# A hybrid decoder step: first tiles group by group, HGRN sample tokens as 32-column weight tiles, triangle steps later in the emitted order

## The chip, the cores and the metric

The kernel runs on one core of one Trainium2 chip. The metric is the device time of one execution in microseconds (us). A core has five engines that run their own instruction streams in order: PE (TensorE, matrix products; PEld is its weight load), DVE (VectorE), ACT (ScalarE), POOL (GpSimd) and SP (SyncE, which here only issues transfers). They wait for each other through semaphores.

## The reference

One layer of a decoder with three kinds of mixing heads side by side, for 256 prompt tokens and 8 sample sequences of 8 tokens each (T = 320 columns). All in float32.

```
hn   = rms_norm(x, norm_mix)                      # x: 320 tokens x 2048
proj = hn @ w_in                                  # 2048 x 6656: 52 output tiles of 128 columns
y_rw = rwkv7_mix(proj[:, :2560], ...)             # 12 heads x 64, as 6 pairs; needs a triangular inverse per 64-token chunk
y_hg = hgrn2_mix(proj[:, 2560:5632], ...)         # 6 heads, state 128 x 128
y_lr = rglru_mix(proj[:, 5632:], ...)             # 512 channels
x    = x + concat(y_rw, y_hg, y_lr) @ w_out       # 16 output tiles
hn   = rms_norm(x, norm_ffn)
gate, val = split(hn @ ffn_w_up)                  # 2 x 5632 columns, conv of width 3 on the gate
x    = x + (silu(conv(gate)) * val) @ ffn_w_down
y    = rms_norm(x, norm_final)

# inside hgrn2_mix, per head and chunk:
o_inter = einsum('bthk,bhkv->bthv', q * exp(b), S)    # the state's share; for sample tokens S is the given state_hgrn
```

## The kernel before

**Products.** Channels lie on the 128 partitions, tokens in the free dimension. A float32 product is made of three: the weight and the input are each split into a rounded high part (ACT, `S.copy` or `S.activation`) and the rest (DVE, the difference), called wh, wl and xh, xl. A tile of 128 output columns takes, for each 128 rows of the input, wh with xh (line 198), wh with xl (line 199) and wl with xh (line 205). A weight chunk is eight such 128 x 128 blocks, 512 KB, so a chunk makes 24 of these large matmuls and an input-projection tile (two chunks) makes 48. Large matmuls of 320 columns are 9600 of PE's matmuls; all others (the "aux" ones) belong to the heads and are plain float32, for which the trace shows two records per matmul.

**Order.** `gemm` emits a tile's matmuls; after every fourth step and every chunk it calls `tick`, which advances generator functions that wait in queues (`QUEUES`): "r" for the chunks of an RWKV pair (`rwkv_chunks`), "f" for its operands, "n" for its norm, "h" for an HGRN head, "l" for the RG-LRU, "y" for the splits ahead of the output projection. A generator yields a number of estimated microseconds (`L_FRONT`, `L_SUB`, `L_EV` ...) to wait on an emission clock that large matmuls (`GEMM_COST`) and aux steps (`AUX_COST`) push on. So these numbers set where in the instruction streams the small work stands; the scheduler of the framework then makes each engine's order from it, and may let neighbours pass each other unless `tc.keep_in_program_order` forbids it. `ORDER` runs pair 0, head 0, pair 1, head 1 and so on, then the RG-LRU pairs.

**Start.** SP loads half chunks of the first weights (`raw`) and most of the 16 input tiles xr; POOL loads every fourth xr, then prm (all small parameters) and cst (constant matrices). ACT's split of an input tile scales it by a column of prm (`nmix`). The first two output tiles (`ps_0`, `ps_1` in `aux_r` buffers: decay/learning-rate and gate inputs of RWKV) are computed in two halves of eight steps. The squares of xr are summed for the RMS norm, one matmul with ones (line 370) adds over partitions, and `rstd` (a square root, then a reciprocal on DVE) scales every projected tile when it is read out of PSUM. Tiles are read by `shifted` (lines 335 to 352, through one `ext` buffer) or `projected`. The projection tiles use two `acc` buffers in turn; `aux_r` has four buffers, `aux_h` two.

**RWKV pair.** `shifted` tiles k, r, v; `rwkv_operands` (first matmuls line 446, then 466); `rwkv_chunks` with the score matmuls (lines 540, 550), masks into mt1 and mt2 on DVE, and the inverse of the 16 x 16 diagonal triangles: mt1 is written to DRAM (`dn`), its diagonal blocks are read as 40 rows (`n16`), 30 small DVE steps (lines 573, 575) build the inverse, which goes by DRAM (`du`) into `Us`. The next reader of `Us` is the transposition at line 648, emitted `L_SUB` after the step ahead of it. `rwkv_norm` (lines 787, 794, 804) follows.

**HGRN head.** `hgrn_steps` makes decayed scores in growing block sizes (lines 871, 875, copied into `at` by DVE at lines 872, 876), then the output `ps_o`:

```
PE.matmul(ps_o[:, TP:T], vt[0:64, 2, :], at[0:64, TP:T], start=True, stop=False, skip_group_check=True)
for m in range(SB):
    PE.matmul(ps_o[:, TP + m * ST:TP + (m + 1) * ST], s0[m // 4][:, m % 4, :], eb[:, m * ST:(m + 1) * ST],
              start=False, stop=True, skip_group_check=True)
```

The first (line 963) is the sample tokens' own share, on 64 rows of the array. The loop (line 965) adds the states' share: for each of the eight sequences its 128 x 128 state is the weight and its eight tokens `eb` (q times exp of the decay) are the moving columns.

Of the kernel before, what the change touches and what calls it, by code (L numbers as in the profile page):

```python
# [66 lines left out]
def kernel(ctx: ExitStack, tc: tile.TileContext, i: dict, o: dict):  # L67
# [200 lines left out]
    for k in range(NK):
        if k % 4 == 0:
            split_weights(2 * (k // 8), slice(k % 8, k % 8 + 4))  # L270
        a, b = split_tiles(k)
        split(xr[k], a, b, pc("nmix", k))
        xh.append(a)
        xl.append(b)
        if k % 4 == 3:
            split_weights(2 * (k // 8) + 1, slice(k % 8 - 3, k % 8 + 1))
# [80 lines left out]
    def rwkv_front():  # L357
        ssq = et("ext", T)

        def squares(ks):  # L360
            for k in ks:
                add_square(ssq, xr[k], k, lambda: rp.tile([P, T], F32, tag="c", name="sq", bufs=BC))
# [7 lines left out]
        PE.matmul(ps_n[:, :T], ones, ssq, start=True, stop=True)  # L370
# [1038 lines left out]
```

## Time and profile before

| what | value |
|---|---|
| median of 3 runs | 1648.94 us (1647.66 to 1649.54) |
| profiled execution, its own time | 1651.69 us |
| its span, first to last instruction | 1649.9 us |
| mean granted TensorE clock | 0.992 |
| PE busy | 1613.8 us, 98% of the span, 11508 matmul records |
| DVE, ACT, POOL busy | 983.7, 827.9, 154.8 us |
| DMA | 238.86 MB, mean 145 GB/s |

A record of PE shows from when a matmul ran to its modelled end; records overlap, so the distance from one start to the next is what a matmul costs in a stream. "idle before" is the time that an engine stood still ahead of an instruction, with what ended it. The granted clock is 1.00 or 0.50 in any short stretch.

### The profile page before, as it was taken

The numbers are of one execution on the slowest core, as the hardware profiler recorded it, in microseconds if no ns is written. First come the engines' busy times: TensorE is split into PE (matmuls) and PEld (weight loads), VectorE is DVE, ScalarE is ACT, GpSimd is POOL, SyncE is SP. The second block draws the span as 40 slices with busy tenths as digits, with TensorE's granted clock in tenths as the row PEclk, the third lists the DMA queues.
The fourth block names the chain that finished last, engine by engine and source line by source line (L and its number), as shares of the span: only waits on it lengthen the run. The fifth ranks groups of instructions, "written<-read, shape, count | busy, mean of one in ns | idle before, by whom it ended". The sixth has DMA issues, their size and how long they took to land.

```text
span 1649.9 us, 29024 instructions
## 1 busy us (share of the span) xinstructions
PE 1613.8 (98%) x11508; PEld 1567.1 (95%) x11508; DVE 983.7 (60%) x1952; ACT 827.9 (50%) x1293; POOL 154.8 (9%) x369
## 2 busy tenths in 40 slices
PE   7999999999999999999999999999999999999996
PEld 7888998999899899999999999999999999999996
DVE  7777777877777656555555554343455555554444
ACT  7675767676766874443434433323343343344441
POOL 2001010101012210010000000000000000010000
PEclk9999999999999999999999999999999999999998
DMA  7434443434343455444444544555544444455553
GB/s 255 151 123 123 121 132 113 131 113 131 113 128 120 149 158 165 147 157 154 149 146 152 151 146 144 151 154 151 153 150 146 152 154 151 146 155 153 146 153 105
DMA packets 87103, 238.86 MB, mean 145 GB/s; under 512 B 16568, under 2 KB 30312, under 8 KB 86968
## 3 DMA queue, kind: packets, MB, share of 16 engines
q1 hardware_dynamic: 82072, 221.67, 44.1%
q0 software_dynamic: 4896, 15.35, 2.9%
q8 instruction: 90, 1.47, 0.4%
q14 instruction: 45, 0.37, 0.1%
HBM read 225.62 MB, written 11.37 MB: 144 GB/s over the span
## 4 chain that ended last, share of the span: by engine, by line
PE 90%; DVE 3%; DMA 3%; ACT 3%; issue 1%; SPq 0%; DVEq 0%; ACTq 0%
PE acc L205 27%; PE acc L198 27%; PE acc L199 26%; DMA U<-du 1%; PE aux_r L665 1%; PE aux_h L875 1%; DVE wl L174 1%; PE aux_h L965 1%; DMA xr<-in_xT 1%; DMA du<-u 1%; PE aux_r L198 0%; PE aux_h L998 0%; PE aux_r L199 0%; ACT wh L173 0%; DVE x L1234 0%
## 5 line engine op out<-in xcount | busy, mean ns | idle before, releaser
L173 ACT CAST wh<-raw 128x1024 fp32r<-128x1024 f32 (+2 forms) x412 | 421.1, 1023 | 518.9 <-PE acc L199 315.8
L198 PE MATMUL acc<-xh,wh 128*128 128x320 f32 x2208 | 668.4, 316 | 3.2 <-DVE ext L342 3.2
L199 PE MATMUL acc<-xl,wh 128*128 128x320 f32 x2208 | 658.0, 311 | 0.0
L174 DVE TENSOR_TENSOR wl<-raw,wh 128x1024 fp32r<-128x1024 f32 (+2 forms) x412 | 489.5, 1189 | 238.5 <-ACT wh L173 109.0
L198 PEld LDWEIGHTS acc<-xh,wh 128*128 128x128 f32 x2208 | 416.8, 189 | 10.9 <-issue 7.8
L199 PEld LDWEIGHTS acc<-xl,wh 128*128 128x128 f32 x2208 | 417.4, 189 | 2.1
L205 PE MATMUL acc<-xh,wl 128*128 128x320 f32 x2208 | 382.5, 314 | 0.2 <-DVE wl L174 0.2
L205 PEld LDWEIGHTS acc<-xh,wl 128*128 128x128 f32 x2208 | 337.9, 190 | 4.2 <-issue 1.0
L198 PE MATMUL acc<-hh,wh 128*128 128x320 f32 x704 | 208.2, 311 | 0.0
L199 PE MATMUL acc<-hl,wh 128*128 128x320 f32 x704 | 207.9, 308 | 0.0
L198 PEld LDWEIGHTS acc<-hh,wh 128*128 128x128 f32 x704 | 132.4, 188 | 0.0
L199 PEld LDWEIGHTS acc<-hl,wh 128*128 128x128 f32 x704 | 132.2, 188 | 0.0
L205 PE MATMUL acc<-hh,wl 128*128 128x320 f32 x704 | 118.9, 309 | 0.0
L1196 POOL COPY ncch<-fe 128x18 f32<-128x18 f32 x44 | 49.6, 1127 | 653.4 <-DVE fe L1195 653.4
L205 PEld LDWEIGHTS acc<-hh,wl 128*128 128x128 f32 x704 | 107.1, 188 | 0.0
L1206 DVE TENSOR_TENSOR fv<-acc,rstd 128x320 f32<-128x320 f32 x44 | 21.6, 492 | 98.1 <-PE acc L205 98.1
L1194 DVE TENSOR_TENSOR fe<-acc,rstd 128x256 f32<-128x256 f32 x44 | 18.7, 425 | 99.2 <-PE acc L205 99.2
L214 ACT CAST hh<-fv 128x320 fp32r<-128x320 f32 x44 | 20.3, 461 | 96.9 <-DVE fv L1208 96.9
L198 PE MATMUL acc<-yhl,wh 128*128 128x320 f32 x224 | 66.2, 310 | 0.5 <-ACT yhl L214 0.5
L199 PE MATMUL acc<-yhl,wh 128*128 128x320 f32 x224 | 66.2, 309 | 0.0
L1201 DVE SCALAR_TENSOR_TENSOR fc<-fe,prm,fc 128x336 f32<-128x336 f32 x88 | 49.8, 565 | 1.6
L1199 ACT ACTIVATE fc<-fe,prm 128x336 f32<-128x336 f32 x44 | 29.5, 669 | 35.1 <-DVE fe L1195 35.1
(406 smaller groups left out, 1650.5 us busy)
## 6 DMA issues: line engine op xcount, KB each, us to landing
raw<-in_w_up SPq DMA_DIRECT2D x176, 512.0 KB, 3.5
raw<-in_w_in SPq DMA_DIRECT2D x100, 512.0 KB, 3.7
raw<-in_w_dn SPq DMA_DIRECT2D x64, 512.0 KB, 3.6
raw<-in_w_out SPq DMA_DIRECT2D x32, 512.0 KB, 3.8
raw<-in_w_dn SPq DMA_DIRECT2D x32, 384.0 KB, 3.4
out_s_hgrn<-hs POOLq DMA_DIRECT2D x12, 256.0 KB, 3.8
hs<-in_hs POOLq DMA_DIRECT2D x10, 256.0 KB, 3.8
x<-in_xT POOLq DMA_DIRECT2D x16, 160.0 KB, 2.8
```

Of the source, the lines that this page charges most:

```text
L173: S.copy(wh[:, ks, :], raws[n][:, ks, :])
L174: V.tensor_tensor(wl[:, ks, :], raws[n][:, ks, :], wh[:, ks, :].bitcast(F32), op=ALU.subtract)
L198: PE.matmul(ps[:, :T], wh[:, k, :], xh[k0 + k], start=st, stop=False)
L199: PE.matmul(ps[:, :T], wh[:, k, :], xl[k0 + k], start=False, stop=False)
L205: PE.matmul(ps[:, :T], wl[:, k, :], xh[k0 + k], start=False, stop=en)
L214: S.copy(xh, src)
L665: PE.matmul(ps[q, b * 64:(b + 1) * 64], lhs[q, b, q], r[q], start=True, stop=True)
L1194: V.tensor_tensor(e[:, 2:258], ps[:, 0:TP], rstd[:, 0:TP], op=ALU.mult)
L1196: G.tensor_copy(ncch[:, j], e[:, 248:EX].rearrange("p (b s) -> p b s", s=10)[:, :, 8:10])
L1199: S.activation(c[:, 0:N], e[:, 0:N], AF.Identity, scale=pc("fw", 3 * j), bias=pc("fb", j))
L1201: V.scalar_tensor_tensor(c[:, 0:N], e[:, m:m + N], pc("fw", 3 * j + m), c[:, 0:N], op0=ALU.mult, op1=ALU.add)
L1206: V.tensor_tensor(val, ps[:, :T], rstd, op=ALU.mult)
```

## The change

1. **Input.** All 16 xr come through SP's queue in groups of four, each group between the halves of the weight chunks that use it; the raw buffer of chunk 3 is taken from another pool. The nmix columns of prm get a small load of their own on ACT's queue at the very start; prm and cst themselves are loaded from ACT's queue after the second and the third group. What reads prm early (`omu`, `hgrn_bounds`, `lru_rates`) stands later in the program.
2. **First tiles.** `first_tiles` makes the first two tiles group by group: for four input tiles all 12 matmuls of tile 0, then all 12 of tile 1. Three float32 matmuls on a tile of zeros (`NIDLE`) stand ahead of them. The squares are spread between the groups. After the first tiles comes pair 0's k tile, and only then the norm's matmul. Pair 0's v tile uses an `aux_r` buffer.
3. **HGRN sample tokens.** `eb` is now four weight tiles of 32 columns (16 tokens of two sequences, and 16 zero columns). Each multiplies the two states of its sequences side by side (256 moving columns) into 32 partitions of PSUM. DVE picks each token's own state's half with two masked operations (`bm2`) into `oi`; one matmul with a selection matrix (`sel`) adds it transposed to `ps_o`. The tokens' own share uses all 128 rows.
4. **Emission.** `L_SUB` goes from 5.0 to 13.5; pair 0's operands start `L_FIRST` = 11 later and end `L_FIRST_OPS` = 4 later; the norm's first wait is `L_NORM` = 2.5 instead of 1.5.
5. **Stores.** The 16 last stores of yT alternate between ACT's and SP's queue.

```
+    idle = rp.tile([P, T], F32, tag="c", name="idle", bufs=BC)
+    V.memset(idle, 0.0)
+    ps_i = aux_h()
+    for n in range(NIDLE):
+        PE.matmul(ps_i[:, :T], idle[:, 0:P], idle, start=True, stop=True)
     S.activation(warm, eps_norm, AF.Sqrt)
+    nmix = cp.tile([P, NK], F32, tag="nmix", name="nmix")
+    S.dma_start(out=nmix, in_=i["prm"][:, PRM["nmix"]:PRM["nmix"] + NK])
-    for k in range(NK):
-        if k % 4 == 0:
-            load(2 * (k // 8), slice(k % 8, k % 8 + 4))
-        t = yp.tile([P, T], F32, tag=f"y{k}", name="xr")
-        (G if k % 4 == 3 else SY).dma_start(out=t, in_=i["xT"][k])
-        if k == 0:
-            G.dma_start(out=prm, in_=i["prm"])
...
-    G.dma_start(out=cst, in_=i["cst"])
+    raws[3] = rp.tile([P, 10, P], F32, tag="big", name="raw3", bufs=BB)
+    for g in range(4):
+        ks = slice(4 * g % 8, 4 * g % 8 + 4)
+        if g < 3:
+            load(2 * (g // 2), ks)
+        for k in range(4 * g, 4 * g + 4):
+            t = yp.tile([P, T], F32, tag=f"y{k}", name="xr")
+            SY.dma_start(out=t, in_=i["xT"][k])
+            xr.append(t)
+        if g == 3:
+            load(2, ks)
+        load(2 * (g // 2) + 1, ks)
+    for g in range(4):
...
+        if g:
+            squares(range(4 * g - 4, 4 * g) if g < 3 else ())
+        if g == 1:
+            tc.keep_in_program_order(S.dma_start(out=prm, in_=i["prm"]))
+        if g == 2:
+            tc.keep_in_program_order(S.dma_start(out=cst, in_=i["cst"]))
...
+    def first_tiles():
+        pss = [aux_r(), aux_r()]
+        for g in range(4):
+            for n, ps in enumerate(pss):
+                wh, wl = splits[2 * (g // 2) + n]
+                for k in range(4 * g, 4 * g + 4):
+                    PE.matmul(ps[:, :T], wh[:, k % 8, :], xh[k], start=(k == 0), stop=False)
+                    PE.matmul(ps[:, :T], wh[:, k % 8, :], xl[k], start=False, stop=False)
+                for k in range(4 * g, 4 * g + 4):
+                    PE.matmul(ps[:, :T], wl[:, k % 8, :], xh[k], start=False, stop=(k == NK - 1))
...
     def rwkv_front():
-        ps_0, ps_1 = (gemm((8,), xh, xl, last=False, ps=aux_r()) for _ in range(2))
-        squares(range(0, NSQ))
-        for ps in (ps_0, ps_1):
-            gemm((8,), xh, xl, k0=8, first=False, ps=ps)
-        squares(range(NSQ, NK))
+        ps_0, ps_1 = first_tiles()
+        tc.keep_in_program_order(V.tensor_scalar(omu, ...))
+        squares(range(8, NK))
+        ps_k = gemm(W_CHUNKS, xh, xl)
         ps_n = aux_h()
-        PE.matmul(ps_n[:, :T], ones, ssq, start=True, stop=True)
+        tc.keep_in_program_order(PE.matmul(ps_n[:, :T], ones, ssq, start=True, stop=True))
...
-            box[name] = shifted(n + 3 * p)
+            ps = gemm(W_CHUNKS, xh, xl, ps=aux_r()) if p == 0 and name == "v" else ps_k
+            ps_k = None
+            box[name] = shifted(n + 3 * p, ps)
...
-        eb = rp.tile([P, TS], F32, tag="eb", name="eb", bufs=1)
-        S.activation(eb, b[:, TP:T], AF.Exp)
-        V.tensor_tensor(eb, q[:, TP:T], eb, op=ALU.mult)
+        ev = eb[:, :, 0:16]
+        S.activation(ev, b[:, TP:T].rearrange("p (g s) -> p g s", s=16), AF.Exp)
+        V.tensor_tensor(ev, q[:, TP:T].rearrange("p (g s) -> p g s", s=16), ev, op=ALU.mult)
...
+        ps = aux_h()
+        for g in range(4):
+            PE.matmul(ps[32 * g:32 * g + 32, 0:TP], eb[:, g, :],
+                      s0[g // 2][:, 2 * (g % 2):2 * (g % 2) + 2, :].rearrange("p a b -> p (a b)"), start=True, stop=True)
+        oi = rp.tile([P, P], F32, tag="hcr", name="oi", bufs=1)
+        V.tensor_scalar(oi, ps[:, 0:P], cc("bm2")[:, 0:1], None, op0=ALU.mult)
+        V.scalar_tensor_tensor(oi, ps[:, P:TP], cc("bm2")[:, 1:2], oi, op0=ALU.mult, op1=ALU.add)
...
-        PE.matmul(ps_o[:, TP:T], vt[0:64, 2, :], at[0:64, TP:T], start=True, stop=False, skip_group_check=True)
-        for m in range(SB):
-            PE.matmul(ps_o[:, TP + m * ST:TP + (m + 1) * ST], s0[m // 4][:, m % 4, :], eb[:, m * ST:(m + 1) * ST],
-                      start=False, stop=True, skip_group_check=True)
+        PE.matmul(ps_o[:, TP:T], vt[:, 2, :], at[:, TP:T], start=True, stop=False, skip_group_check=True)
+        PE.matmul(ps_o[:, TP:T], oi, cc("sel"), start=False, stop=True, skip_group_check=True)
...
-        SY.dma_start(out=o["yT"][n], in_=y)
+        (S if n % 2 else SY).dma_start(out=o["yT"][n], in_=y)
...
-L_SUB = 5.0
+L_SUB = 13.5
+L_NORM = 2.5
```

**How rows move.** ACT at the very start, before (the line is that of the kernel, then the operation, written and read tiles, shape):

```order
L255 ACT_TABLE_LOAD
L255 ACTIVATE warm<-eps_t 128x1
L1010 ACTIVATE lrut<-prm 128x4
L173 CAST wh<-raw 128x512
L217 ACTIVATE xh_139<-xr,prm 128x320
L217 ACTIVATE xh_151<-xr,prm 128x320
```

And in the changed kernel:

```order
L263 DMA nmix<-in_prm 128x16
L261 ACT_TABLE_LOAD
L261 ACTIVATE warm<-eps_t 128x1
L173 CAST wh<-raw 128x512
L217 ACTIVATE xh_146<-xr,nmix 128x320
L249 ACTIVATE ext<-xr 128x320
L217 ACTIVATE xh_150<-xr,nmix 128x320
```

The instruction that reads prm (line 1010, of `lru_rates`) has left the front of ACT's queue, a small load and squares (line 249) have come in.

PE at the end of HGRN head 0, before:

```order
L960 MATMUL aux_h<-at,vt 128x128
L961 MATMUL aux_h<-a_1207,vt 128x128
L962 MATMUL aux_h<-at,vt 128x128
L963 MATMUL aux_h<-at,vt 128x64
L965 MATMUL aux_h<-eb,hs_1036 128x8 x4
L965 MATMUL aux_h<-eb,hs_1038 128x8 x4
L198 MATMUL acc<-xh_161,wh 128x320
```

In the changed kernel the states' matmuls stand 16 large matmuls ahead of the output's (line numbers are the new file's; L729 and L732 are steps of pair 0):

```order
L729 MATMUL aux_r<-rq,U 128x128 x4
L732 MATMUL aux_r<-ws,U 128x64
L999 MATMUL aux_h<-hs_964,eb 32x256 x2
L999 MATMUL aux_h<-hs_966,eb 32x256 x2
L198 MATMUL acc<-xh_236,wh 128x320
```

```order
L1010 MATMUL aux_h<-at,vt 128x128
L1011 MATMUL aux_h<-a_1147,vt 128x128
L1012 MATMUL aux_h<-at,vt 128x128
L1013 MATMUL aux_h<-at,vt 128x64
L1014 MATMUL aux_h<-cst,oi 128x64
L198 MATMUL acc<-xh_146,wh 128x320
```

Sixteen narrow records have become eight of 256 columns and two of 64, and L1014 now needs `oi` from DVE. In the other heads 16 large matmuls lie between L999 and L1014 too, 8 in the last.

DVE in pair 0's triangle steps (the small t and u rows), before:

```order
L573 TENSOR_TENSOR t_862<-n_860,u_861 40x15
L906 TENSOR_TENSOR x<-b 128x40x4
L575 TENSOR_TENSOR u_861<-u_861,t_862 40x15
L174 TENSOR_TENSOR wl<-raw,wh 128x1024
L910 TENSOR_TENSOR qk<-hk,e 128x40x4
L910 TENSOR_TENSOR qk<-hq,e 128x40x4
L911 TENSOR_TENSOR b<-b 128x40x4
L906 TENSOR_TENSOR x<-b 128x16x8
L933 TENSOR_TENSOR eb<-hq,eb 128x64
L911 TENSOR_TENSOR b<-b 128x16x8
L872 COPY_PREDICATED at<-msk,aux_h 128x128
```

And in the changed kernel:

```order
L975 TENSOR_TENSOR eb<-hq,eb 128x4x16
L611 TENSOR_TENSOR t_909<-n_907,u_908 40x64
L174 TENSOR_TENSOR wl<-raw,wh 128x1024
L613 TENSOR_TENSOR u_908<-u_908,t_909 40x8x8
L914 COPY_PREDICATED at<-msk,aux_h 128x128
L611 TENSOR_TENSOR t_909<-n_907,u_908 40x63
L613 TENSOR_TENSOR u_908<-u_908,t_909 40x7x9
```

The first copy of head 0's scores stood behind the last triangle step and stands now in the middle of them. On PE, the large matmuls between a pair's L540 (now L578) and L648 (now L686) go from 162 to 144 for pair 0, from 145 to 152 for pair 1, and from 145 to 160 for pairs 2 to 5; those from pair 0's L540 to head 0's first L871 (now L913) go from 136 to 80.

More of the change, by code (lines that the diff above doesn't have):

```diff
@@ L267, with squares @@
-    G.dma_start(out=cst, in_=i["cst"])
[L268 to L276, printed above, removed]
-    state["raw"] = state["split"] = 4
-    prefetch()
+    ssq = et("ext", T)
+    def squares(ks):
+        for k in ks:
+            add_square(ssq, xr[k], k, lambda: rp.tile([P, T], F32, tag="c", name="sq", bufs=BC))
@@ new lines @@
+    raws[3] = rp.tile([P, 10, P], F32, tag="big", name="raw3", bufs=BB)
[11 more added lines that the diff above has]
+    for g in range(4):
+        ks = slice(4 * g % 8, 4 * g % 8 + 4)
+        split_weights(2 * (g // 2), ks)
+        for k in range(4 * g, 4 * g + 4):
+            a, b = split_tiles(k)
+            split(xr[k], a, b, nmix[:, k:k + 1])
+            xh.append(a)
+            xl.append(b)
+        split_weights(2 * (g // 2) + 1, ks)
+        if g:
[4 more added lines that the diff above has]
+            tc.keep_in_program_order(S.dma_start(out=cst, in_=i["cst"]))
@@ new lines @@
+    state["raw"] = state["split"] = 4
+    def first_tiles():
[6 more added lines that the diff above has]
+                    PE.matmul(ps[:, :T], wh[:, k % 8, :], xl[k], start=False, stop=False)
+                for k in range(4 * g, 4 * g + 4):
+                    PE.matmul(ps[:, :T], wl[:, k % 8, :], xh[k], start=False, stop=(k == NK - 1))
+            state["clock"] += 24 * GEMM_COST
+            if g % 2:
+                for n in range(2):
+                    splits.pop(state["used"])
+                    state["used"] += 1
+                prefetch()
+        return pss
@@ L357, in rwkv_front @@
     def rwkv_front():
[L358 to L362, printed above, removed]
-        ps_0, ps_1 = (gemm((8,), xh, xl, last=False, ps=aux_r()) for _ in range(2))
-        squares(range(0, NSQ))
-        for ps in (ps_0, ps_1):
-            gemm((8,), xh, xl, k0=8, first=False, ps=ps)
-        squares(range(NSQ, NK))
+        ps_0, ps_1 = first_tiles()
+        tc.keep_in_program_order(V.tensor_scalar(omu, prm[:, PRM["mu"]:PRM["mu"] + 20], -1.0, 1.0, op0=ALU.mult, op1=ALU.add))
+        squares(range(8, NK))
+        ps_k = gemm(W_CHUNKS, xh, xl)
         ps_n = aux_h()
-        PE.matmul(ps_n[:, :T], ones, ssq, start=True, stop=True)
+        tc.keep_in_program_order(PE.matmul(ps_n[:, :T], ones, ssq, start=True, stop=True))
         rstd_from(ps_n, rstd, rp.tile([P, T], F32, tag="c", name="rstd_s", bufs=BC))
@@ L522, in rwkv_operands @@
         free(r_own)
+        if p == 0:
+            yield L_FIRST_OPS
         box["ops"] = AR, BK, ep, rk
@@ L833, in hgrn_head @@
         box["g"] = projected("hg")
+    eb = mp.tile([P, 4, 32], F32, tag="eb", name="eb")
+    G.memset(eb, 0.0)
     def hgrn_steps(n, box):
@@ L1135, in y_steps @@
             yield L_Y
-    rwkv_front()
-    hgrn_bounds()
-    lru_rates()
+    ps_k = rwkv_front()
     spawn("y", y_steps())
     for kind, n in ORDER:
-        {"r": rwkv_pair, "h": hgrn_head, "l": lru_pair}[kind](n)
+        if (kind, n) == ("h", 0):
+            hgrn_bounds()
+        if (kind, n) == ("h", 2):
+            lru_rates()
+        if (kind, n) == ("r", 0):
+            rwkv_pair(0, ps_k)
+        else:
+            {"r": rwkv_pair, "h": hgrn_head, "l": lru_pair}[kind](n)
     force(lambda: yl[7] is not None)
```

23 lines of the change are left out of this document (13 added, 10 removed).

## The prediction

> **What bounds the kernel now.** I read the page first, then stages of equal role (windows), then what PE waits for, then the timelines of the places that the change touches.
>
> ```profile
> span 1649.9 us, 29024 instructions
> PE 1613.8 (98%) x11508; PEld 1567.1 (95%) x11508; DVE 983.7 (60%) x1952; ACT 827.9 (50%) x1293; POOL 154.8 (9%) x369
> PE 90%; DVE 3%; DMA 3%; ACT 3%; issue 1%; SPq 0%; DVEq 0%; ACTq 0%
> ```
>
> PE is busy for 98% of the span and is 90% of the chain that ended last. So time goes only where PE has less to do, waits less, or runs at a better clock. The stages say where that can be (columns: us of the stretch, then busy time of PE, PEld, DVE, ACT and POOL with counts, the granted clock, DMA share, GB/s):
>
> ```profile
> 0.00:7.56 7.56, 0.00 (x1) 0.01 (x1) 0.88 (x7) 2.72 (x6) 5.54 (x15) 1.00 0.73 215
> 7.56:28.26 20.70, 19.26 (x96) 18.11 (x97) 17.56 (x33) 18.32 (x38) 3.02 (x14) 1.00 0.80 277
> 43.20:57.79 14.59, 11.37 (x54) 10.55 (x55) 6.42 (x21) 11.96 (x19) 1.06 (x7) 0.77 0.33 123
> 57.79:200.00 142.21, 138.49 (x1152) 126.78 (x1151) 111.30 (x313) 96.35 (x187) 15.82 (x41) 1.00 0.41 126
> 200.00:380.00 180.00, 177.98 (x1424) 163.19 (x1423) 137.68 (x383) 125.96 (x239) 23.31 (x58) 1.00 0.41 122
> 380.00:560.00 180.00, 176.53 (x1382) 162.43 (x1381) 132.11 (x346) 122.81 (x235) 29.87 (x55) 0.97 0.42 129
> 560.00:1636.40 1076.40, 1075.35 (x7310) 1071.71 (x7308) 554.69 (x802) 439.31 (x559) 72.19 (x169) 1.00 0.49 149
> ```
>
> The output projection and the feed-forward part (from 560 on) leave PE 1.05 us idle in 1076, and the change leaves them alone but for the last stores. All gains lie before 560: PE starts at 7.56, the first two tiles take 20.7 us, and from 57.79 to 560 PE idles 3.72 + 2.02 + 3.47 = 9.2 us. What ended the idle time (total, times, longest):
>
> ```profile
> PE aux_r L198 <- ACT xh L217: 8.9, 2, 7.6
> PE aux_r L648 <- DMA U<-du: 5.6, 6, 1.3
> PE acc L198 <- DVE ext L342: 3.2, 1, 3.2
> PE aux_r L787 <- DVE y L772: 0.7, 1, 0.7
> ```
>
> **Term 1, the start (to the end of pair 0's v tile).** Rows of ACT, PE and DMA at the start:
>
> ```profile
> 6.33 0.20 ACT L1010 ACTIVATE lrut<-prm 128x4 f32<-128x4 f32 x1 [4.09 <-DMA prm<-in_prm]
> 6.44 0.60 ACT L173 CAST wh<-raw 128x512 fp32r<-128x512 f32 x1
> 6.94 1.92 ACT L217 ACTIVATE xh<-xr,prm 128x320 fp32r<-128x320 f32 x4
> ...
> 16.66 2.34 PE L205 MATMUL aux_r<-xh,wl 128*128 128x320 f32 x8
> ...
> 20.55 1.55 ACT L252 ACTIVATE sq<-xr 128x320 f32<-128x320 f32 x4
> ...
> 23.86 1.34 PE L205 MATMUL aux_r<-xh,wl 128*128 128x320 f32 x8
> ```
>
> ```profile
> xr<-in_xT SPq DMA_DIRECT2D x3, 160.0 KB, 2.7
> ```
>
> ```profile
> 8.00:16.00 8.00, 6.56 (x22) 5.57 (x22) 6.63 (x14) 6.30 (x14) 2.58 (x11) 1.00 1.05 377
> ```
>
> ACT sits behind L1010, which waits for prm until 6.33. In the new order the first things ACT needs are an 8 KB nmix load, half a weight chunk (issued at about 0.7) and xr 0 (1.2): at 2.7 us to landing, 3.5 and 3.9. So ACT starts near 3.5. Until the last input is split it has 8 half casts (0.5 apart, 6.44 to 6.94), 16 xh (1.92/4 = 0.48), 8 squares (1.55/4 = 0.39), and two DMA issues, about 0.5 each by SP's rows at the end: 4.0 + 7.7 + 3.1 + 1.0 = 15.8, so 19.3. The 4.7 MB of x and of the first four chunks need about 16 us (1.4 MB by 8 us as now at some 280 GB/s, then 377 GB/s), so ACT is the limit. DVE's last pieces and some 14 matmuls at the warm 0.147 follow: first tiles done near 22 instead of 28.26. PE itself isn't the limit: eight matmuls take 2.34 us when slow and 1.34 when fast, and three idle matmuls, 3.3 us at the slow rate (0.55 warm each, from the 256-column row below), fill the time until the first split, so that the fast rate can begin within the first group or two and not at 18.8.
>
> Then k, the norm's sum, r and v: 144 x 0.147 + 0.6 = 21.7, to 43.8. Before, the same point is 57.79, of which some 1.3 must come off for matmuls of 320 columns that now stand later (L446 on two halves and L466, by the same 0.55): 56.5. This takes the 3.20 stall as gone:
>
> ```profile
> 33.54 0.70 PE L370 MATMUL aux_h<-ext,cst 128*128 128x320 f32 x2
> ...
> 47.70 0.60 PE L198 MATMUL acc<-xh,wh 128*128 128x320 f32 x1 [3.20 <-DVE ext L342]
> ```
>
> ```profile
> 46.30:53.10 6.80, 5.40 (x20) 5.43 (x21) 3.63 (x8) 5.34 (x8) 0.62 (x4) 0.50 0.26 90
> ```
>
> PE stood there because both acc buffers held unread tiles, and 6.8 us at half clock followed. Now v goes to an aux_r buffer, and k's buffer is needed only at 43.8. The old lag from L370 (33.54) to that release was 14.2 us; from the new L401 at about 29.3 it ends at 43.5. **Term 1: 12.7, taken as 12.5**; ends 7.5 (stall and slow stretch come back, 3.2 + 2) and 15. Moving prm, cst and the POOL loads costs nothing: cst is read first at 29. What is late next is ACT itself.
>
> **Term 2, the sample tokens of HGRN.** Start to start, since a row's length holds latency:
>
> ```profile
> 273.15 0.66 PE L717 MATMUL aux_r<-mt,vsw 128*64 128x128 f32 x8
> 273.74 0.45 PE L724 MATMUL aux_r<-bkt,pq 64*64 64x64 f32 x12
> ...
> 275.62 0.38 PE L743 MATMUL aux_r<-qv,bkt 128*128 128x128 f32 x2
> 275.83 0.60 PE L760 MATMUL aux_r<-ex,bks 128*128 128x256 f32 x2
> 276.27 0.33 PE L875 MATMUL aux_h<-qk 128*128 128x64 f32 x2
> ```
>
> ```profile
> 381.13 0.43 PE L963 MATMUL aux_h<-at,vt 64*128 64x64 f32 x2
> 381.49 1.95 PE L965 MATMUL aux_h<-eb,hs 128*128 128x8 f32 x16
> 383.30 0.39 PE L198 MATMUL acc<-xh,wh 128*128 128x320 f32 x1
> ```
>
> L963 and L965 take 2.17 us per head (two records a matmul). New: the 64-column matmuls L1013 and L1014 on the full array, at most 0.22 each like L743, and the four 32-column tiles of 256 columns, where one takes 0.44 (L760). No row shows four such tiles. The nearest, L717, has two 64-column tiles with their own moving data: four matmuls in 0.59 where four times L743 would be 0.84, with the pair's records starting together. By that all four run in about 0.44 + 0.2 for entering and leaving: 1.1 per head, 1.1 less, six heads 6.6. With no overlap they are 1.76 + 0.2, so 2.4, and six heads lose 1.4. I take 6.6, since L717 is nearest. DVE's two added reads of 128 columns lie beside PE, which has 3.3 us of other work between L999 and L1014; without that cover they cost what rival (d) says.
>
> [...]
>
> **Term 3, the clock.**
>
> ```profile
> 380.80:384.20 3.40, 3.40 (x28) 3.21 (x27) 3.40 (x9) 1.01 (x2) 1.58 (x3) 1.00 0.49 159
> 384.20:387.60 3.40, 3.40 (x15) 3.20 (x13) 0.94 (x2) 2.33 (x2) 0.65 (x1) 0.50 0.43 152
> ...
> 548.00:551.40 3.40, 3.40 (x14) 3.20 (x14) 0.16 (x1) 2.51 (x3) 0.00 (x0) 0.51 0.48 182
> ```
>
> Three heads are followed by 3.4 us at half clock (the second of them, from 466.1, reads alike), 1.7 us lost each. The stretch ahead has no idle PE but all of L965: 8 columns per weight load. With L965 gone I take the three drops as gone, 5.1, and charge one new drop at term 4's place: **3.4**, ends 0 and 5.1.
>
> **Term 4, waits of pair and head.** From L540 to L648 of a pair stand 145 large matmuls for pairs 1 to 5; now 152, then 160, which is 1.0 to 2.2 us more, and of the norm's matmuls up to 1.1 too. The longest wait there is 1.3. So pairs 1 to 5 lose their 5.2, and L787's 0.7 goes (24 large matmuls or more ahead of it, not 16). Pair 0 gets worse:
>
> ```profile
> 93.77 0.49 PE L871 MATMUL aux_h<-e,f 128*128 128x128 f32 x2 [1.34 <-DVE at L872]
> ...
> 99.00 0.63 PE L648 MATMUL aux_r<-cst,U 128*128 128x128 f32 x4 [0.40 <-DMA U<-du]
> ```
>
> Its distance falls from 162 to 144, and head 0's first score matmuls (L871, now L913) come 80 after L540 instead of 136, while DVE is still in the 30 small triangle steps: the copy L914 stands behind 14 of them and two weight splits. By my count of DVE's rows it ends some 2.3 us late, and U some 1.4: 3.7 against 1.7 now. Everything on PE waits behind these. **Term 4: 5.2 + 0.7 - 2.0 = 3.9**, ends -2 (pair 0 waits 8) and 7.
>
> **Term 5, the last stores.**
>
> ```profile
> 1639.67 7.77 SPq L1237 DMA_DIRECT2D out_yT<-x  x16
> ```
>
> ```profile
> 1645.20 0.54 DVE L1236 SCALAR_TENSOR_TENSOR x<-x,prm,rstd 128x320 f32<-128x320 f32 x1
> ```
>
> SP issues 16 stores in 7.77, 0.49 apart, the last near 1647.0, though DVE is done at 1645.74. With two queues the last goes at about 1645.8: **1.2** (0 if a store issued by ACT takes as long as two of SP's, 1.3 at best).
>
> **Sum.** 12.5 + 6.6 + 3.4 + 3.9 + 1.2 = 27.6. The profiled execution took 1651.69 (1.8 around its span), 2.75 over the median; it would take 1624.1, and the median 1648.94 becomes 1621.3.
>
> **Rivals.** (a) The four tiles run one after another: term 2 is -1.4, 1629.3. L717's shared starts speak against it, four streams instead of two for it. (b) The clock drops aren't L965's: term 3 is -1.7, 1626.4. For it: PE is busy throughout the stretch ahead. Against: all three drops follow L965 at once. [...] (c) ACT's start slips, or the accumulator stall returns: term 1 is 7.5, 1626.3; for it, 43.5 against 43.8 is a thin margin. (d) Slower: L1014 waits for oi, which DVE makes from L999's result, and all of PE's queue stands behind it. A wait like the one at 47.70 costs 3.2 plus half of 6.8, 6.6 per head, 39.6 for six: 1621.3 + 39.6 = 1660.9. It decides from 4.6 us per head. Against: between L999 and L1014 PE has 3.3 us of work or more, DVE's rows ahead of oi come to about 1.8. (e) The start is bound by DMA as before and pair 0 takes the rest: no change, about 1647.
>
> **How the numbers follow.** Forecast 0.57 (own range 1614 to 1626), (a) 0.12, (b) 0.11, (c) 0.13, (d) 0.04, (e) 0.03. The range 1611 to 1632 takes in terms 1 and 4 at their upper ends and any one of (a) to (c). A difference under 0.2% (3.3 us) can't be told from none: faster 0.93, same 0.03, slower 0.04.
>
> **What would show it.** Right: ACT's first cast near 3.5, first tiles done at 21 to 23, no wait at the hq tile, L999's eight records starting in fours, no clock of 0.5 after the heads, no L686 wait past pair 0, stores ending 1.2 earlier. Wrong: L999 over 1.5 us per head, PE idle ahead of L1014, or DVE as releaser in each head.

## The result, and the profile after

The kernel after takes 1634.16 us (median of 4 runs, 1633.52 to 1635.15) against 1648.41 for the kernel before (4 runs, 1647.66 to 1649.54): ratio 0.9914, 95% interval 0.9896 to 0.9931. That is 14.3 us less; 27.6 were forecast, and 1634.16 lies above the range. Four later runs of the same kernel (experiment 8) gave 1635.74 against 1649.42, 13.7 less.

The profiled executions differ by more, 1651.69 to 1633.52, 18.2 us: the one of before lay 2.7 over its median, the one of after was the fastest of its four. The page of the kernel after, its lines on the span, the engines and the chain:

```profile
span 1631.8 us, 28987 instructions
PE 1604.3 (98%) x11478; PEld 1549.6 (95%) x11478; DVE 984.9 (60%) x1965; ACT 821.9 (50%) x1289; POOL 147.9 (9%) x364
PE 89%; DVE 5%; ACT 4%; issue 1%; DMA 1%; SPq 0%; DVEq 0%; ACTq 0%
```

PE is the bound as before; DVE's share of the chain rose from 3% to 5%. The stages of the kernel after, cut at the first matmul of x, the end of the first tiles and the end of pair 0's v tile with L482, then at 200, 380 and 560 us (columns as in the prediction):

```profile
4.88:23.55 18.67, 17.95 (x97) 16.36 (x97) 15.87 (x32) 15.32 (x32) 1.70 (x8) 1.00 0.96 339
23.55:47.39 23.84, 22.76 (x152) 21.70 (x150) 19.13 (x32) 15.37 (x24) 6.22 (x19) 1.00 0.73 234
47.39:200.00 152.61, 146.22 (x1195) 132.83 (x1193) 117.40 (x343) 107.83 (x207) 15.32 (x45) 1.00 0.39 124
200.00:380.00 180.00, 177.47 (x1436) 159.61 (x1432) 141.37 (x399) 122.92 (x236) 23.81 (x57) 1.00 0.41 126
380.00:560.00 180.00, 178.10 (x1406) 161.44 (x1405) 137.88 (x363) 129.70 (x254) 27.98 (x67) 1.00 0.42 129
```

No stage shows half clock any more (the seventh column was 0.77 and 0.97 in two stages). But PE idles 6.4 us between 47 and 200, more than in the same part before. What PE waits for:

```profile
PE aux_r L781 <- DVE sbd L794: 3.2, 4, 2.0
PE aux_h L917 <- DVE at L918: 1.9, 3, 0.6
PE aux_h L913 <- DVE at L914: 1.6, 1, 1.6
...
PE aux_r L502 <- ACT kn L499: 1.3, 1, 1.3
PE aux_h L401 <- DVE ext L253: 1.1, 1, 1.1
...
PE aux_r L703 <- DVE T L695: 0.6, 1, 0.6
```

The wait for U's transfer, 5.6 us before, is gone at all six pairs, and so are the 3.2 at the hq tile and the 0.7 at the norm. In their place stand waits for DVE at L781, L917, L401 and L703 that the kernel before did not have; L913's is the old 1.34 at L871, a little longer.

### The profile page after: what moved, and what is told of

Read it like the earlier page. It is cut to its first block, busy times and chain, and to the rows that moved or that the text cites. A ratio compares the mean times of both kernels' runs of the same rounds, so it can differ in the third digit from the quotient of the medians.

```text
span 1631.8 us, 28987 instructions
## 1 busy us (share of the span) xinstructions
PE 1604.3 (98%) x11478; PEld 1549.6 (95%) x11478; DVE 984.9 (60%) x1965; ACT 821.9 (50%) x1289; POOL 147.9 (9%) x364
## 4 chain that ended last, share of the span: by engine, by line
PE 89%; DVE 5%; ACT 4%; issue 1%; DMA 1%; SPq 0%; DVEq 0%; ACTq 0%
PE acc L198 27%; PE acc L205 27%; PE acc L199 26%; DMA raw<-in_w_in 1%; PE aux_r L703 1%; PE aux_h L917 1%; DVE wl L174 1%; ACT wh L173 0%; DVE x L1287 0%; PE aux_h L913 0%; PE aux_h L1046 0%; PE aux_r L781 0%; ACT L505 0%; PE aux_r L482 0%; PE aux_r L578 0%
## 5 line engine op out<-in xcount | busy, mean ns | idle before, releaser
L198 PE MATMUL acc<-xh,wh 128*128 128x320 f32 x2192 | 661.2, 315 | 0.0
L199 PE MATMUL acc<-xl,wh 128*128 128x320 f32 x2192 | 650.4, 310 | 0.0
L198 PEld LDWEIGHTS acc<-xh,wh 128*128 128x128 f32 x2192 | 411.6, 188 | 8.0 <-issue 5.5
L199 PEld LDWEIGHTS acc<-xl,wh 128*128 128x128 f32 x2192 | 412.0, 188 | 1.2
L205 PE MATMUL acc<-xh,wl 128*128 128x320 f32 x2192 | 375.6, 313 | 0.8 <-DVE wl L174 0.8
L205 PEld LDWEIGHTS acc<-xh,wl 128*128 128x128 f32 x2192 | 331.9, 188 | 6.8 <-issue 3.0
L205 PE MATMUL acc<-hh,wl 128*128 128x320 f32 x704 | 118.8, 308 | 0.0
L205 PEld LDWEIGHTS acc<-hh,wl 128*128 128x128 f32 x704 | 107.1, 187 | 0.0
```

The source lines that it names most:

```text
L198: PE.matmul(ps[:, :T], wh[:, k, :], xh[k0 + k], start=st, stop=False)
L199: PE.matmul(ps[:, :T], wh[:, k, :], xl[k0 + k], start=False, stop=False)
L205: PE.matmul(ps[:, :T], wl[:, k, :], xh[k0 + k], start=False, stop=en)
```

## Where the time went

From the trace's rows I took, for each PE record, the time to the next record's start, less what PE stood idle and less half of what fell into stretches at half clock, and grouped it. The stretch is the same work in each kernel: from the end of pair 0's v tile to large matmul 2400, the end of the mixing part (us of one profiled execution each; the kernels in the middle are experiments below):

| | before | HGRN alone | start alone | delays alone | after, old delays | after |
|---|---|---|---|---|---|---|
| whole stretch | 516.9 | 513.3 | 525.2 | 518.7 | 518.2 | 510.4 |
| waits of PE | 9.2 | 12.6 | 14.7 | 8.9 | 17.6 | 10.8 |
| lost at half clock | 5.1 | 3.4 | 6.8 | 3.4 | 3.4 | 0.0 |
| HGRN output (L960 to L965; L999 to L1014) | 17.6 | 10.9 | 17.6 | 17.6 | 11.2 | 9.7 |
| other small matmuls, and what large ones take over 0.147 | 167.9 | 169.2 | 169.0 | 171.7 | 168.8 | 172.8 |
| large matmuls at 0.147 | 317.1 | 317.1 | 317.1 | 317.1 | 317.1 | 317.1 |

Between the two profiles: start 10.4 (57.79 to 47.39), HGRN output 7.9, half clock 5.1, waits -1.6, other small matmuls -4.9, last stores 1.1, the rest of the kernel 0.2. Together 18.2, as seen. The second row from below had no term in the prediction. Its 4.9 come mostly with the longer delays (3.8 alone). The matmuls are the same; their neighbours in PE's queue have changed. With the delays alone, L625's twelve records take 3.45 us from start to start instead of 1.78, and in five of six pairs the matmuls of L998 now follow them where large ones did. That small matmuls stand further apart is not enough to explain it: the kernel after with the old delays has 201 separate groups of them, the one with the delays alone 199, and takes 2.9 less. What a neighbour costs was not tested by itself.

## The experiments

Times are medians, set against runs of the kernel before on the same chip. A line number is that of the run's own kernel: close to before's where it was made from before, and to after's otherwise (L914 in experiment 13 is after's L913).

**1. The kernel before, again.**

> The kernel before, unchanged, run and profiled again. Theory A: the three stretches of half clock that term 3 counts (5.1 us) are no fixed part of the kernel before; its profiled execution of 1651.69, 2.7 over the median, had more of them than the median run has. Then the granted clock of its runs is mostly above 0.992 (0.994 to 0.995, since one stretch of 3.4 us at half clock is 0.1% of the span), and a new profile shows none or one of them, perhaps at other heads. Rival B (the prediction's term 3): each follows the 16 narrow matmuls of L965 by rule; then all runs read 0.992 and the new profile shows the same three, from 384, 466 and 548.

1649.11 against 1649.04, ratio 1.000 (0.9991 to 1.0008). Granted clock of its runs 0.992 to 0.995, mean 0.9935; those at 0.995 took 1646.3 to 1647.1, the one at 0.992 took 1649.66. The new profile has four stretches at half clock again: one after the stall at the hq tile, and three after heads, from 138.2, 302.0 and 465.9 where the first profile had 384.2, 466.1 and 548.0. Theory A falls: such drops are in nearly every run. Rival B holds in part: they follow L965, but at other heads each time.

**2 to 4. Each part alone.**

```diff
 HGRN alone: before, with eb/sel/bm2, L999, oi and L1014 of the kernel after
 start alone: before, with first_tiles, the input order, k ahead of the norm, v in aux_r, L_FIRST, L_FIRST_OPS
 delays alone: before, with
-L_SUB = 5.0
+L_SUB = 13.5
+L_NORM = 2.5
```

> The kernel before with the HGRN part of the change alone (sample tokens as weights of four 32-column tiles, the two-mask sum, the sel matmul). Theory A: only the matmuls that go count, 1.1 to 1.3 us a head: 6.6 to 8 us, so 1640.5 to 1642 against 1648.4. Rival B: the three drops of the clock go with L965 in every run, 5.1 more: 1635.3 to 1637. Rival C (the four tiles add waits elsewhere): 1645 or more.

> The kernel before with the start of the change alone (one ordered input queue, first tiles in turn, three idle matmuls, k ahead of the norm, v in an aux_r buffer, later constants, pair 0's two added delays); HGRN loop, the delays of the triangles and of the norm, and the last stores as before. Prediction's term 1: 12.5 less, 1636. Theory A, from the trace after (v tile ends near 46.6 where 43.8 was forecast): 8 to 10 less, 1638.5 to 1640.5, less what pair 0 and head 0 then wait more (up to 2).

> The kernel before with the later reading of the triangles alone (the delay ahead of the U matmul 13.5 in place of 5.0, the norm's 2.5 in place of 1.5). Prediction's term 4 for pairs 1 to 5: 5.2 + 0.7 less, 1642.5. Theory A: the U waits go, but PE then waits elsewhere (for the product sbd at the next step, at head 0 and in the norm), so that 0 to 2 are left: 1646.5 to 1648.5. Rival C: slower by up to 2.

Against 1649.04: HGRN alone 1644.41 (ratio 0.9972, 0.9961 to 0.9982); start alone 1650.73 (1.0009, 0.9995 to 1.0024); delays alone 1652.10 (1.0023, 1.0014 to 1.0031). With 1.1 for the stores the parts add up to 0.9 less, where the whole gives 14 less. HGRN alone lies between its theory A (1642 at most) and rival C (1645), and rival B is out; the other two miss every value expected of them.

The start alone reaches the end of v's tile 10.0 us earlier and has kept 1.8 of it at the end of the mixing part. Its waits are 14.7 (8.6 of them for U), its clock falls to 0.9912 on average, and its runs spread from 1644.7 (clock 0.993) to 1658.7 (0.987). In the kernel with the delays alone, PE's waits name what took U's place:

```profile
PE aux_h L875 <- DVE at L876: 2.7, 5, 0.6
PE aux_r L583 <- DVE mt L546: 2.0, 1, 2.0
PE aux_r L446 <- DMA lw<-in_lw: 1.7, 1, 1.7
PE aux_r L743 <- DVE sbd L756: 1.5, 4, 0.4
```

No U wait is left, and the sum of waits is 8.9 as against 9.2: they only changed their names. That part of theory A holds. Its time does not: the kernel got 3.1 slower, more than rival C's 2, and the table has 3.8 more for the other small matmuls, which no theory had. HGRN alone shows rival (d) of the prediction in small among PE's waits, once per head:

```profile
PE aux_h L975 <- DVE oi L964: 2.6, 6, 0.5
```

**5 to 8. One part undone, and the kernel after again.**

```diff
 5: after, with the old HGRN sample loop
 6: after, with
-L_SUB = 13.5
-L_NORM = 2.5
+L_SUB = 5.0
+L_NORM = 1.5
 7: before, with HGRN's new part, the later delays and the two store queues
 8: after, unchanged
```

> The kernel after with the old HGRN sample loop (start, later triangles and stores stay). Alone, the start gave +1.7 us, the later triangles +3.1, HGRN -4.6 and the stores come to -1.0 by the trace: together -0.8, where the whole change gave -14.3. Theory A: the parts meet in the clock. PE's work, waits and 1.7 us per stretch of half clock add up, and such a stretch follows where a wait or L965's narrow matmuls fall into one 3.4-us window. So here 7.6 - 1.4 us of PE work come back, and about three stretches: 1634.2 + 6.2 + 5.1 = 1645.5, granted clock 0.993 to 0.994. Rival B (costs of the parts simply add to before): 1649.0 + 1.7 + 3.1 - 1.0 = 1652.8. Rival C (only work comes back, the clock stays 0.996): 1640.4.

> The kernel after with the old delays (5.0 ahead of the U matmul, 1.5 in the norm). Theory A: PE's small matmuls cost 3.2 less as they stand together again, but the U waits come back (14.7 of waits as with the start alone, against 10.8) and with them two to four stretches of half clock: 1634.2 - 3.2 + 3.9 + 3.4 to 6.8 = 1638.3 to 1641.7, clock 0.993 to 0.995. Rival B (parts add): 1649.0 + 1.7 - 4.6 - 1.0 = 1645.1. Rival C (the later triangles bring nothing, as alone): 1631 to 1634.

> The kernel before with HGRN's new tokens, the later triangles and the stores on two queues: the kernel after without its start. Theory A: 10.4 us at the start and the stall at the hq tile with its 3.4 to 6.8 us of half clock come back: 1634.2 + 10.4 + 1.7 to 3.4 = 1646.3 to 1648.0, clock 0.994 to 0.995 and no half clock between 60 and 560. Rival B (parts add): 1649.0 - 4.6 + 3.1 - 1.0 = 1646.5; the clock tells the two apart: by B there are still drops at heads or pairs.

> The kernel after, unchanged, timed in more runs. Theory A: with no L965 and no wait over 2.1 us its runs have none or one stretch of half clock: granted clock 0.996 to 0.997 and a spread of 2 us, where the kernel before spreads over 7 (1646.4 to 1653.3 in 31 runs). Rival: the four runs seen were lucky, and clocks of 0.993 and times to 1640 occur.

Against 1649.42: 1644.00 (0.9969, 0.9958 to 0.9980), 1642.46 (0.9962, 0.9948 to 0.9976), 1644.04 (0.9965, 0.9953 to 0.9977) and 1635.74 (0.9916, 0.9904 to 0.9929). Taken from the whole, HGRN is worth 8.3, the delays 6.7 and the start 8.3. The simple sum (rival B) is wrong by 8.8, 2.6 and 2.5 us; theory A is near for 5 and 6, and too pessimistic by 2 for 7, whose profile has drops after waits at 97 and 152, which A had excluded. Of 8 A's clock is wrong too (0.994 to 0.996, two drops in the profile, a spread of 4.4 us), and so is its rival: no run came near 0.993 or 1640.

So the delays cost 3 us alone and bring 7 beside the other two. The waits of the kernel after with the old delays show why:

```profile
PE aux_r L686 <- DMA U<-du: 9.4, 5, 4.1
PE aux_h L1014 <- DVE oi L1003: 2.3, 5, 0.5
```

With a shorter start and shorter heads, the U waits grow from 5.6 to 9.4 (8.6 with the start alone, 6.6 with HGRN alone), and oi is late at five heads. The delays take both away.

**What a drop of the clock follows.** In the kernel after, run twice, the same place with and without a drop (experiment 8, then the profile of the result):

```profile
133.46:136.87 3.41, 1.37 (x11) 1.15 (x10) 2.18 (x4) 0.29 (x2) 0.00 (x0) 1.00 0.26 65
136.87:140.29 3.42, 3.42 (x16) 3.42 (x15) 0.91 (x3) 1.29 (x3) 1.08 (x2) 0.50 0.25 98
```

```profile
133.70:137.11 3.41, 2.18 (x17) 2.18 (x18) 2.05 (x6) 0.64 (x2) 0.34 (x1) 1.00 0.51 151
137.11:140.52 3.41, 3.41 (x24) 3.25 (x23) 2.05 (x4) 0.88 (x2) 0.74 (x2) 1.00 0.10 31
```

The 2.05-us wait at L781 is in both. In the first the 3.41-us window holds all of it, PE is busy 1.37 us, and the next window runs at 0.50; in the second the window begins 1.0 us later against the work, PE is busy 2.18, and nothing happens. The changes of the clock recorded in these profiles stand on a grid of 3.413 us: in the kernel before, from 18.97 to 551.45, they lie 8, 2, 97, 1, 23, 1, 23 and 1 times 3.413 apart, and from one drop to the next there are 48 and 48 of them after the heads of experiment 1, 15 in experiment 8 above and below. Where the grid begins differs from run to run (133.46 and 133.70 above). For each grid window before 600 us I estimated the time in which PE streamed columns, from the pitches of its records at full clock: 0.147 us for 320 columns (L205), so 0.459 ns a column for the large matmuls, and 0.109 for 128 (L743), so 0.85 for the others. Over the 17 profiles of this case, 2886 windows at full clock:

| share of the window streamed | windows | followed by half clock |
|---|---|---|
| under 0.38 | 39 | 38 |
| 0.38 to 0.40 | 8 | 4 |
| 0.40 to 0.60 | 69 | 0 |
| above | 2770 | 0 |

The expectation of experiment 9, written after ten profiles (28 drops), has this bound already. In the seven profiles from there on, 15 windows lie under 0.40, and 14 of them were followed by a drop; no other window was. These are counts over this kernel's versions; what makes the drops was not shown. The bound isn't sharp: at L913 the same two runs have windows that are alike, at 0.37 both, and only experiment 8 has a drop behind it (its rows first):

```profile
82.26:85.67 3.41, 1.82 (x12) 1.54 (x12) 3.07 (x13) 0.68 (x1) 0.00 (x0) 1.00 0.69 233
85.67:89.09 3.42, 3.42 (x16) 3.42 (x15) 1.84 (x11) 2.82 (x6) 0.00 (x0) 0.50 0.16 66
```

```profile
82.50:85.91 3.41, 1.80 (x12) 1.31 (x11) 3.25 (x14) 0.22 (x2) 0.00 (x0) 1.00 0.73 235
85.91:89.32 3.41, 3.41 (x24) 3.08 (x22) 3.12 (x17) 3.38 (x6) 0.00 (x0) 1.00 0.28 113
```

The sixteen eight-column records of L965 keep PE busy for 1.81 us a head, 0.11 apart, and by this estimate stream for 0.007 us each, so in this sum they count like a wait. If the grid is shifted over each trace, windows under 0.39 are expected, by the same estimate, 3.6 and 4.2 times a run for the kernel before (two profiles), 0.9 times for the kernel after; 3.41 us at half clock cost 1.7 us each time. Most of the runs' spread goes with it: of the 63 runs of the kernel before that the experiments were set against, those at a mean clock of 0.995 took 1646.4 to 1647.2, those at 0.990 1653.3 to 1653.7. Some of it does not, since at 0.993 alone they lie between 1647.6 and 1650.4.

**9. L965 in two halves, in the kernel before.**

```diff
         for m in range(SB):
+            if m == SB // 2:
+                yield L_HG
             PE.matmul(ps_o[:, TP + m * ST:TP + (m + 1) * ST], ...
```

> The kernel before with the eight narrow sample matmuls of each HGRN head in two halves of four, some 16 large matmuls between them; the same matmuls otherwise. Theory A: a 3.41-us window in which TensorE streams columns for less than about 0.39 of the time is followed by one at half clock. The traces so far have 28 such drops in 1691 windows, all after windows under 0.40, and four windows under 0.40 without one. A head's whole loop (1.81 us) makes 1.0 to 2.3 us of window positions under 0.39, six heads 2.2 to 2.6 drops a run; half a loop makes none. So 2.2 to 2.6 times 1.7 less, 1.0 more for the extra gaps: 1645 to 1646.5, clock 0.995, no half clock after heads, only the stretch at the hq tile's stall. Rival B (half clock needs a pause of PE; the narrow matmuls are not its cause): 1649 to 1650, clock 0.993, drops at heads as before.

1662.92 against 1650.54 (1.0081, 1.0061 to 1.0102): slower by 12, so both expectations of the time are wrong. What A said of the clock holds in its one profile: L965 leaves no place under 0.39, and the two drops of the mixing part each come after another place, the wait for U. One of them, and PE's first wait:

```profile
169.09:172.50 3.41, 1.43 (x10) 1.27 (x10) 0.88 (x3) 1.28 (x4) 0.00 (x0) 1.00 0.68 240
172.50:175.92 3.42, 3.42 (x39) 2.96 (x40) 2.44 (x6) 1.41 (x7) 0.00 (x0) 0.50 0.25 57
```

```profile
PE aux_r L648 <- DMA U<-du: 11.5, 6, 2.4
```

The extra yield moved everything behind it, and the U waits doubled from 5.6 to 11.5; the five from pair 1 on, 2.0 to 2.4 long, each make a new place under 0.39. Sorted as in the table, the mixing part has 5.8 more of waits and 4.8 more of other small matmuls. That profile was the fastest of its six runs; what the others lost beyond it is open.

**10 and 12. Longer delays where waits are left.**

```diff
 12: after, with
-L_ST = 0.5
+L_ST = 1.5
 10: the same, and
-L_HG0 = 12.0
+L_HG0 = 15.0
```

> The kernel after with two delays longer: L_ST 1.5 for 0.5 (the state steps of a pair, L781, some 16 large matmuls apart and not 8) and L_HG0 15 for 12 (the first scores of a head, L913, 24 large matmuls later). Theory A (what is left of the waits is a matter of distance): the waits at L781 (2.05 + 0.37 + 0.36 + 0.38) and at L913 (1.61) go, and with them both places where the clock can drop (0.9 a run): 4.8 + 1.5 = 6.3 less than after's 1634 to 1635.7, so about 1628.5 to 1630, clock 0.997. Rival B (as with the triangles: a wait that is taken away comes back behind the next in DVE's queue): 1633 to 1636.

> The kernel after with L_ST 1.5 for 0.5 alone. Theory A: L781's waits (3.2) go, and the drop that can follow the longest (0.6 a run, 1.0): 4.2 less, 1630 to 1631.5; L913's 1.61 stays. Rival B: 1633 to 1636, with a new wait behind DVE's L1023, which stood 3.33 us for ACT's hrs ahead of the sbd copy that L781 waited for.

Number 10 took 1660.21 against 1650.54 (1.0063, 1.0047 to 1.0078), number 12 took 1636.17 (0.9920, 0.9904 to 0.9936). Theory A falls in both. In 10 rival B is off too, by 24 us; in 12 its time is near, though the waits that came are others than it named. In 10 PE waits most for these:

```profile
PE aux_r L640 <- ACT sqy L834: 12.2, 5, 2.4
PE aux_r L781 <- DVE sbd L794: 4.4, 5, 0.9
```

A new wait of 2.45 us at each of five pairs, for ACT and not for DVE, each followed by a drop in the profile: 27 us later than after at the end of the mixing part. In 12 the old wait shrank and two others came, by PE's waits:

```profile
PE aux_h L913 <- DVE at L914: 5.0, 6, 1.6
PE aux_r L703 <- DVE T L695: 3.2, 5, 0.6
PE aux_r L781 <- DVE sbd L794: 2.3, 5, 0.6
```

**11. No idle matmuls.**

```diff
-NIDLE = 3
+NIDLE = 0
```

> The kernel after without the three idle matmuls at its start. Theory A (ACT bounds the start, PE is not its limit): full clock begins at 14 to 16 us and not at 10.8, the first tiles end 0 to 1 later than 23.3: 1634 to 1636. Rival B (PE's clock bounds the start): 2 to 3 later, 1636.5 to 1638.5.

1633.79 against 1650.54 (0.9903, 0.9886 to 0.9919), the same as with them. The record of the clock begins with the change to full rate, at 11.97 instead of 10.79 (theory A had said 14 to 16); until then the large matmuls start 0.26 apart or more, and not 0.147. The first tiles end at 23.77 instead of 23.55. In the eleven profiles with the new start, the first full rate begins between 5.1 and 13.6, and the first tiles end between 23.1 and 24.5, not later where it begins later (24.02 after 10.34, 23.79 after 13.58). So theory A holds in the main: PE's clock did not bound the start here.

**13 to 15. The norm's sum later, head 0's scores later, the norm's delay undone.** All three without idle matmuls.

```diff
 13: after, with
         ps_k = gemm(W_CHUNKS, xh, xl)
+        ps_r = gemm((8,), xh, xl, last=False)
         ps_n = aux_h()
...
+        gemm((8,), xh, xl, k0=8, first=False, ps=ps_r)
 14: after, with
-        yield L_HG0
+        yield L_HG0 + (3.0 if n == 0 else 0.0)
 15: after, with
-L_NORM = 2.5
+L_NORM = 1.5
```

> The kernel after without idle matmuls (1633.8 as measured) and with the norm's sum L401 in the middle of pair 0's r tile, 24 large matmuls later. Theory A: its wait of 1.08 us for DVE's last sum of squares goes and nothing else moves: v's tile ends 1.1 earlier, 1632.5 to 1633. Rival B: everything that rstd holds up (the k tile's reading, pair 0's operands) starts 2.5 later, and 1 to 3 us come back as waits at L502, L588 or L913: 1634 to 1637.

> The kernel after without idle matmuls and with head 0's first scores L913 24 large matmuls later (L_HG0 15 for head 0, 12 for the others as before). Theory A: the 1.61 us wait at L913 and the drop that follows it in about a quarter of the runs go: 1633.8 - 1.6 - 0.4 = 1631.8. Rival B (a change in one place of the order sets all later places anew, as with e10): waits elsewhere, 1634 or more; the longest wait and the places under 0.39 tell it.

> The kernel after without idle matmuls and with the norm's delay at 1.5 as before, the triangles' at 13.5. If the triangles' delay carries the 6.8 us that both delays bring here: 1633 to 1635 and no wait at L825 over 0.7. If the norm's carries part: 1636 or more, with a wait of 0.7 or more at L825 in several pairs.

Against 1648.68: 1640.60 (0.9952, 0.9940 to 0.9964), 1632.83 (0.9904, 0.9891 to 0.9918) and 1634.18 (0.9910, 0.9895 to 0.9925). In 13 the wait at L401 went, yet the mixing part ended 7.5 us later than in the kernel after. Large matmul 672 came 11.9 earlier, but only because the order had moved: 310 records of small matmuls stand ahead of it instead of 366. Among its waits is one of 3.2 us that was not there:

```profile
PE aux_h L914 <- DVE at L915: 4.1, 3, 2.4
PE aux_r L799 <- DVE gbd L767: 3.2, 1, 3.2
```

That is rival B, and more than it said. In 14 the wait at head 0 only moved, but the 2.0 at L781 went, by its waits of PE:

```profile
PE aux_h L917 <- DVE at L918: 1.9, 3, 0.6
PE aux_h L913 <- DVE at L914: 1.7, 1, 1.7
PE aux_r L703 <- DVE at L918: 1.5, 1, 1.5
PE aux_r L781 <- DVE sbd L794: 1.1, 3, 0.4
```

It lies between theory A and rival B. It is the fastest by its median, but its interval covers that of the kernel after, so no version is shown to be better. 15 shows that the triangles' delay carries the gain of the two: without the norm's, the time is the same and no wait at L825 appears.

## Why the prediction was wrong, by its own steps

**Term 4 is the step that failed: 3.9 less was forecast, about 5 more came** (waits 1.6 more, and 4.9 for small matmuls, of which 1.3 go with HGRN by experiment 2). It took waits that go as time gained, and it put what the new order does to the small matmuls at nothing, without a reason. The prediction priced each wait by how many large matmuls lie ahead of it, and that was right for each: the U waits and the 0.7 went. It did not ask what the freed PE meets next. An example is DVE ahead of L781 in pair 0 of the kernel after, with what ACT does meanwhile:

```profile
132.46 0.49 DVE L1023 TENSOR_TENSOR hrs<-aux_h,hrs 128x320 f32<-128x320 f32 x1 [3.33 <-ACT hrs L1022]
132.87 1.22 DVE L174 TENSOR_TENSOR wl<-raw,wh 128x1024 fp32r<-128x1024 f32 x1
134.00 0.55 DVE L1025 SCALAR_TENSOR_TENSOR yo<-hrs,prm,hg 128x320 f32<-128x320 f32 x1
134.58 0.29 DVE L794 TENSOR_SCALAR sbd<-aux_r,ep 64x64 f32<-64x64 f32 x1
```

```profile
128.83 1.28 ACT L1021 ACT_TABLE_LOAD   x1
...
130.67 1.28 ACT L1022 ACT_TABLE_LOAD   x1
```

PE waits 2.05 us for a copy of 0.29 that stands behind three instructions, the first of which waits 3.33 us for ACT. ACT spends 2.56 us just then on two loads of activation tables, one for each of its two steps of head 0's norm. No run tried to take these away. The prediction named what is queued behind a wait only for head 0 (forecast 2.3 and 1.4 late; PE waited 1.61 at L913, and the U wait it feared did not come). And it set the delays against the waits of the old kernel; beside the new start and the shorter heads they remove 9.4 of U waits and 2.3 of oi waits, and are worth 6.7, but as part of a sum that starts from a worse state.

**Term 1, forecast 12.5.** ACT's first cast was due at 3.5, the first tiles at 22 and the end of v (without L482) at 43.8. The timelines of ACT and PE in the kernel after have:

```profile
3.75 0.62 ACT L173 CAST wh<-raw 128x512 fp32r<-128x512 f32 x1 [1.07 <-DMA raw<-in_w_in]
...
19.74 0.42 PE L308 MATMUL aux_r<-xl,wh 128*128 128x320 f32 x1 [0.56 <-DVE xl L218]
...
31.84 0.81 PE L401 MATMUL aux_h<-ext,cst 128*128 128x320 f32 x2 [1.08 <-DVE ext L253]
```

They came at 3.75, 23.55 and 46.65, 2.85 late: 1.55 at the first tiles, 1.08 at L401, whose sum DVE finished late behind two weight splits of 1.22, 0.2 else. At the first tiles the mis-sized step is the tail: at 19.74 PE had 23 large matmuls left, where the prediction took 14 from about 19.9 on. ACT was not alone in bounding this stage either; between its first cast and 19.95, the end of its last split of x, it waited 1.85 us for loads, and DMA was at 0.96. No wait at the hq tile: the stall of rival (c) did not come back. Against 56.5 that is 9.9 in these two profiles; by the ends of v's tile with L482, six starts of the old kind (55.2 to 57.8, mean 56.4) and ten of the new (46.6 to 48.5, mean 47.4), it is 8.9. Of the start's parts only the idle matmuls (experiment 11) and L401's place (13) were tried apart; the order of the input, the groups, v's buffer and pair 0's two delays were not.

**Term 2, forecast 6.6, was right in kind and size here.** The four tiles overlap, by PE's timeline in head 0 of the kernel after:

```profile
117.74 0.64 PE L999 MATMUL aux_h<-hs,eb 128*32 128x256 f32 x8
118.31 0.41 PE L198 MATMUL acc<-xh,wh 128*128 128x320 f32 x1
...
123.48 0.33 PE L1013 MATMUL aux_h<-at,vt 128*128 128x64 f32 x2
123.65 0.39 PE L1014 MATMUL aux_h<-cst,oi 128*128 128x64 f32 x2
123.84 0.39 PE L198 MATMUL acc<-xh,wh 128*128 128x320 f32 x1
```

Eight records from 117.74 to 118.31, 0.57 us where one tile was taken as 0.44, and 0.36 for L1013 and L1014. So 0.13 came on top of the 0.44; the 0.2 that the prediction added for entering and leaving is shown by no run. The output matmuls take 7.9 less, and some 1.3 come back in what stands around them: 6.6. (Experiment 5 against after gives 8.0 and 1.2; HGRN alone, with oi late at each head, 6.7 and 1.3.) Rival (a) is out. Rival (d) is there at 0.45 us a head with the old delays, in 2 and 6, and gone with the new ones; its point of decision, 4.6, was far.

**Term 3, forecast 3.4.** Its picture, three drops that come with L965 by rule and one new drop, was too fixed: by the estimate of experiment 9 (1.0 to 2.3 us of 3.41) each head gives a chance of 0.3 to 0.7 by where the grid lies. The size stands: an estimated 1.7 to 2.3 drops fewer a run from v's tile on by the shifted grid, 2.9 to 4.0 us. The profile pair shows 5.1, since the profiled run of after had none: that is luck of the phase. Rival (b) is not borne out for L965 (experiment 9), and right in that drops follow waits too (there the wait for U, ahead of 172.50).

**Term 5, forecast 1.2, measured 1.1.** From PE's last end to the span's end 13.5 before and 12.5 after; the last store is issued 0.03 behind DVE's last result, by the timeline's last rows:

```profile
1628.09 0.54 DVE L1289 SCALAR_TENSOR_TENSOR x<-x,prm,rstd 128x320 f32<-128x320 f32 x1
1628.19 0.33 SPq L1290 DMA_DIRECT2D out_yT<-x  x1
1628.66 0.34 ACTq L1290 DMA_DIRECT2D out_yT<-x  x1
```

In sizes for typical runs: 8.9 + 6.6 + 2.9 to 4.0 - 5.2 + 1.1 + 0.2 = 14.5 to 15.6, where 14.3 and 13.7 were measured; the rest is not placed. Why the U waits are longer when the start is shorter was not followed to its first late instruction.

The signs that the prediction named for being right came true all but one (the first tiles ended at 23.55, not by 23), and the time was off all the same: none of them looked at what else PE would wait for, or at the small matmuls.

## What to carry to other kernels

Price a removed wait only after naming what its engine's partner does next: where one queue (here DVE's) feeds many waits, delaying one reader can move the wait to another (in experiment 4 PE's waits came to 8.9 us after 9.2), and a gain at the start is real only if the stages behind it can use it (in experiment 3, 1.8 of 10.0 us were left). Parts of a change to a hand-set order don't add: run each alone and each undone before crediting any of them, and take the result as the part's worth in that order only, since one added yield or two longer delays moved the time by 12 and 26 us here. And set waits and narrow matmuls beside the record of the clock: here 42 of the 47 windows of 3.41 us that streamed under 0.40 by the estimate were followed by half clock, at 1.7 us each, and where the windows lie differs from run to run, so a fair time needs several runs.
